# Modulation of a decoder layer: tiles as they arrive, in four column groups

## The chip, the core and the metric

One core of a Trainium2 chip runs one launch of the kernel. The time is the device time of one execution in microseconds. TensorE (PE in the profile, its weight loads PEld) multiplies; VectorE (DVE) and ScalarE (ACT) work element by element; GpSimd (POOL) and SyncE (SP) mostly issue transfers. Each engine works off its own queue in the order in which the program wrote its instructions, and engines wait for each other by semaphores.

## What is computed

One layer of a decoder over 1056 rows (a prompt of 1024, and 8 sequences of 4), in float32. Cut to what the change touches:

```python
mod = (jax.nn.silu(c) @ p['w_mod'] + p['b_mod'])[:, None, :]     # c: 9 x 1024, w_mod: 1024 x 6144
sh_m, sc_m, g_m, sh_f, sc_f, g_f = jnp.split(mod, 6, axis=-1)
h = rmsnorm(x, p['g_pre_mix']) * (1.0 + sc_m) + sh_m
z = h @ p['w_in']                                                # conv | S5 | q | k | v | gates
...
x = x + g_m * rmsnorm(merged @ p['w_out'], p['g_post_mix'])
hf = rmsnorm(x, p['g_pre_ffn']) * (1.0 + sc_f) + sh_f
```

Only shift and scale of the mixer (the first 2048 columns of mod) are needed before the first dense product; the other two thirds are needed much later.

## The kernel before

Features lie on the partitions, rows of x on the free axis, in three chunks of 352. A dense product is float32 in three float32r matmuls: weight and input are each split in a high and a low part (whi, wlo; hh, hl) and high-high, high-low and low-high are added in one PSUM bank. A weight tile (128 x 1024, 512 KB) is loaded by SP into a ring of three raw tiles, split by ScalarE (whi, line 415) and VectorE (wlo, line 416), and used by three atoms of 24 matmuls, one for each chunk.

The program is a list of atoms, written out in order. run() (line 371) walks through it; before an atom's matmuls it emits the splits and loads that are due. loadable() lets loads run three units ahead of the splits, ready() lets splits run two units ahead of the atoms. An atom's evacuation is emitted behind the next atom's matmuls. Then side.advance() emits steps of side generators (depthwise convolution, attention, sample attention, the S5 preparation), paced by the atoms' cost numbers.

The modulation: w_mod is cut into 12 groups of 512 columns with four tiles of 128 x 1024 each (two blocks of the contraction side by side).

- **First groups 0 to 3** (first_mod, line 541). Tiles come into a ring of six buffers, and each gives two float32 matmuls with 9 stationary columns (cs1) and 512 moving ones; the profile lists a float32 matmul as two instructions, its two passes. After four tiles ScalarE copies the 9 x 512 row, and turn_mod (line 561) transposes it in four pieces and adds the bias.
- **Groups 4 to 11** (mod_atoms, line 569). A tile is a unit like any weight: loaded into the raw ring, split in whi and wlo, then four float32r matmuls of 18 stationary columns (high and low of silu(c), c18). A finished group is copied (line 575), turned by four transposes (line 577), and added up by VectorE. add_mod() puts the 32 units singly between the weights' atoms, by some_mods(), gate_jobs() and conv_job(), down to the S5 stage; after the last, a plain atom may stand between a group's end and its turn.

The entry is ordered by the lists FS and FT (line 683): first_sq squares a chunk of x on ScalarE and adds eight blocks to one on VectorE in three steps; first_stats sums over the partitions by matmuls with a column of ones (four sums of 88 rows each) and takes the reciprocal root in 13 small VectorE instructions; first_norm multiplies (3.15 us of VectorE); first_h applies scale and shift and splits into hh and hl. An entry (c, step, (n, i)) of FS puts the step for chunk c behind first tile i of group n. FT's places are counted by chunk and job of the first three dense weights (conv gate, conv value, first branch gate), which run chunk by chunk. The split of the first weight is emitted once the first modulation is through, that of the second ahead of FT, that of the third at the first dense atom, behind the steps at (0, -1).

SP's queue holds all weight loads, x and the first tiles, in order. A load of the first ring waits until the tile six before it has been used.

## Time and profile before

| | us |
|---|---|
| three runs | 1964.32, 1967.68, 1968.45 |
| median | 1967.68 |
| the profiled execution, its own time | 1960.91 |
| its span, first to last instruction | 1958.8 |
| TensorE busy in the span | 1863.8 |
| VectorE, ScalarE busy | 1337.6, 734.4 |
| mean granted TensorE clock | 0.982 |

The profiled execution lies 6.8 us below the median. A timeline row gives the start and length of a run of like instructions, and in brackets how long the engine stood idle before it and what ended that. Matmuls overlap, so the distance between starts tells their pace; lengths contain the end of the last one.

### The profile page before, as it was taken

To read this page: it belongs to the slowest core of one execution; us is meant where nothing else is said; L and a number is where in the kernel's file an instruction comes from. 1 tells how busy PE (TensorE), PEld (TensorE's weight loads), DVE (VectorE), ACT (ScalarE), POOL (GpSimd) and SP (SyncE) were. 2 spreads that over 40 slices of the span, in tenths; PEclk is the share of its full clock that TensorE was granted. 3 is DMA by queue.
4 is the path that set the end of the run, shared out by engine and by line. 5 is a ranking of instruction groups with operands and counts; after the bars stand their busy time and mean duration, and the time that the engine had idled before them with its cause. 6 is when DMAs were issued, how large, how long until landed. Compare 5 with 4: busy or idle time off the path is not lost. (4 is left out here: it accounts for less than half of the span.)

```text
span 1958.8 us, 33717 instructions
## 1 busy us (share of the span) xinstructions
PE 1863.8 (95%) x13512; PEld 1742.9 (89%) x13512; DVE 1337.6 (68%) x2747; ACT 734.4 (37%) x1442; POOL 230.3 (12%) x386
## 2 busy tenths in 40 slices
PE   8899999999899899999899999999999999999995
PEld 2899799789786789999799999989999999999994
DVE  4777686366366677665786668767777777666786
ACT  3422432432431443222233455434333333464452
POOL 0000001001010023222200001100000000110123
PEclk9999999999999999999999999999999999999997
DMA  7333133223247454324843345542322232685654
GB/s 285 102 104 103 60 108 130 91 98 134 101 143 285 167 177 144 100 96 136 238 134 97 122 159 168 205 162 95 109 99 93 82 117 93 207 274 181 228 189 147
DMA packets 89277, 282.29 MB, mean 144 GB/s; under 512 B 16000, under 2 KB 22240, under 8 KB 86944
## 3 DMA queue, kind: packets, MB, share of 16 engines
q1 hardware_dynamic: 51824, 138.49, 22.1%
q0 software_dynamic: 29952, 115.17, 16.8%
q10 hardware_dynamic: 7344, 26.47, 4.1%
q8 instruction: 106, 1.74, 0.4%
q14 instruction: 51, 0.42, 0.1%
HBM read 212.86 MB, written 68.15 MB: 143 GB/s over the span
## 5 line engine op out<-in xcount | busy, mean ns | idle before, releaser
L308 PE MATMUL z<-mh,wop 128*128 128x264 f32 x2032 | 394.7, 286 | 5.2 <-DVE wop L2051 3.0
L308 PE MATMUL z<-hh,whi 128*128 128x352 f32 x1152 | 379.6, 329 | 3.8 <-ACT whi L415 2.3
L308 PE MATMUL z<-hh,wlo 128*128 128x352 f32 x1152 | 373.0, 324 | 3.1 <-DVE wlo L416 3.1
L308 PE MATMUL z<-hl,whi 128*128 128x352 f32 x1152 | 372.6, 323 | 1.1 <-DVE hl L311 1.1
L308 PE MATMUL z<-ml,wop 128*128 128x264 f32 x1400 | 341.5, 286 | 6.3 <-DVE ml L311 6.2
L308 PEld LDWEIGHTS z<-mh,wop 128*128 128x128 f32 x2032 | 326.6, 191 | 7.1 <-DVE wop L2051 4.2
L416 DVE SCALAR_TENSOR_TENSOR wlo<-raw,whi 128x1024 fp32r<-128x1024 f32 x132 | 160.9, 1222 | 131.1 <-ACT whi L415 124.1
L308 PEld LDWEIGHTS z<-ml,wop 128*128 128x128 f32 x1400 | 242.4, 190 | 7.2 <-DVE ml L311 7.1
L308 PEld LDWEIGHTS z<-hh,whi 128*128 128x128 f32 x1152 | 218.6, 190 | 15.0 <-issue 6.3
L308 PEld LDWEIGHTS z<-hh,wlo 128*128 128x128 f32 x1152 | 218.5, 190 | 3.7 <-DVE wlo L416 3.7
L308 PEld LDWEIGHTS z<-hl,whi 128*128 128x128 f32 x1152 | 218.8, 190 | 3.1 <-DVE hl L311 2.0
L415 ACT ACTIVATE whi<-raw 128x1024 fp32r<-128x1024 f32 x132 | 139.2, 1056 | 180.0 <-PE z L308 164.1
L1534 DVE SCALAR_TENSOR_TENSOR ycv<-cub,vecs,ycv 128x1024 f32<-128x1024 f32 x120 | 153.9, 1282 | 3.1
L2047 ACT ACTIVATE wop<-raw 128x512 fp32r<-128x512 f32 x150 | 91.3, 616 | 148.3 <-PE z L308 117.1
L308 PE MATMUL z<-xa,wop 128*128 128x264 f32 x792 | 108.2, 285 | 0.7 <-DVE wop L2051 0.7
L308 PEld LDWEIGHTS z<-xa,wop 128*128 128x128 f32 x792 | 100.9, 189 | 1.0 <-DVE wop L2051 0.9
L311 DVE TENSOR_TENSOR wop<-raw,wop 128x512 fp32r<-128x512 f32 x90 | 61.9, 688 | 44.5 <-ACT wop L2047 44.4
L308 PE MATMUL z<-mh,whi 128*128 128x264 f32 x288 | 85.8, 298 | 1.3 <-DVE ft L2085 0.7
L308 PE MATMUL z<-ml,whi 128*128 128x264 f32 x288 | 83.1, 288 | 0.0
L308 PE MATMUL z<-mh,wlo 128*128 128x264 f32 x288 | 82.8, 288 | 0.0
L308 PE MATMUL z<-zh,whi 128*128 128x264 f32 x256 | 73.6, 287 | 0.0
L308 PE MATMUL z<-zl,whi 128*128 128x264 f32 x256 | 72.8, 284 | 0.0
(438 smaller groups left out, 3663.1 us busy)
## 6 DMA issues: line engine op xcount, KB each, us to landing
raw<-i_win SPq DMA_DIRECT2D x48, 512.0 KB, 3.6
raw<-i_wfi SPq DMA_DIRECT2D x43, 512.0 KB, 4.1
raw<-i_wfo SPq DMA_DIRECT2D x80, 256.0 KB, 3.3
fd<-ft POOLq DMA_DIRECT2D x22, 792.0 KB, 6.8
raw<-i_wmod SPq DMA_DIRECT2D x32, 512.0 KB, 4.1
gd<-g ACTq DMA_DIRECT2D x24, 528.0 KB, 2.9
g<-gd ACTq DMA_DIRECT2D x24, 528.0 KB, 4.7
ml<-fd POOLq DMA_DIRECT2D x22, 528.0 KB, 6.7
```

Source lines behind the costliest of these rows:

```text
L308: return pe.matmul(out=out, lhsT=lhsT, rhs=rhs, start=start, stop=stop, **kw)
L311: dve.tensor_tensor(out=out, in0=a, in1=b, op=op)
L415: act.activation(out=hi[:, 0:n], in_=raw[:, 0:n], func=AF.Copy, scale=scale)
L416: dve.scalar_tensor_tensor(out=lo[:, 0:n], in0=raw[:, 0:n], scalar=scale, in1=hi[:, 0:n].bitcast(F32), op0=ALU.mult, op1=ALU.subtract)
L1534: dve.scalar_tensor_tensor(out=a_, in0=ub[:, k:k + TP], scalar=wv[:, k:k + 1], in1=a_, op0=ALU.mult, op1=ALU.add)
L2047: act.activation(out=w[:, 0:n], in_=src, func=AF.Copy, scale=scale)
```

## The change

- A tile of the modulation is used as it arrives, in float32, without a split (units with asis). mod_mm gives each of two halves of 256 columns and each of two contraction blocks its own 32 output partitions (0, 32, 64, 96), so four matmuls, eight instructions, of 32 stationary columns go to four column groups of the array. 23 of the 32 stationary columns belong to neighbours and their results are not used.
- A group's turn becomes two float32 matmuls of the copied 128 x 256 row against a constant (C_SUM) that adds the two contraction blocks and turns at once.
- The raw tile stays occupied until its matmuls; loadable() holds back the load that would take its place.
- Placement of the 32 later tiles: two behind each gate weight of the attention stages instead of one, one or two more behind the value weights (some_mods(1 + g // 2)), none after the third attention group. All are through before the S5 preparation, whose tables now share the row's memory (pw).
- The entry: chunk 0 is loaded behind the second tile instead of the third, chunk 1 behind the fourth atom instead of the fifth; squares, sums and norms move in FS; the norm of chunk 1 goes from FS to FT, behind the first h. For chunks 0 and 1 the eight blocks of squares are no longer added by VectorE; first_stats gives all eight to the matmuls.

```diff
--- before.py
+++ after.py
@@ -51,7 +51,8 @@
 C_ID, C_ONE = 0, 128
-NCST = 256
+C_SUM = 256
+NCST = C_SUM + 18
@@ -76,6 +77,9 @@
     cst = np.zeros((128, NCST), f)
     cst[:, C_ID:C_ID + 128] = np.eye(128)
     cst[:, C_ONE:C_ONE + 128] = 1.0
+    for r in range(4):
+        for i in range(9):
+            cst[32 * r + i, C_SUM + 9 * (r // 2) + i] = 1.0
     sel = np.zeros((96, 2, 128), f)
     for g in range(3):
         for p in range(2):
@@ -382,7 +386,7 @@
         def load(v):
             src, n, scale, op, keep = units[v]
-            if op:
+            if op and not op.get('asis'):
                 op['load']()
                 return
             raw = wp.tile([128, 1024], F32, tag="raw", name="raw")
@@ -393,12 +397,17 @@
             op = units[v][3]
             if units[v][4]:
                 return ()
+            if op and op.get('asis'):
+                return ()
             return (('whi', 'wlo')[op['no'] % 2],) if op else ('whi', 'wlo')
         def split(v):
             src, n, scale, op, keep = units[v]
             for t in tags(v):
                 rings[t].append(v)
+            if op and op.get('asis'):
+                parts[v] = raws.pop(v)
+                return
             if op:
                 flush()
                 if v + 1 < len(units) and units[v + 1][3]:
@@ -420,10 +429,14 @@
         def ready(v, i):
             if any(len(rings[t]) >= 3 and last[rings[t][-3]] >= i for t in tags(v)):
                 return False
-            ahead = 6 if units[v][3] else 2
+            ahead = 6 if units[v][3] and not units[v][3].get('asis') else 2
             return v < ahead or first[v - ahead] <= i
-        def loadable():
+        def loadable(i):
+
+            v = nd - 3
+            if 0 <= v < len(units) and units[v][3] and units[v][3].get('asis') and last[v] >= i:
+                return False
             return nd < len(units) and nd < ns + (units[nd][3]['ahead'] if units[nd][3] else 3)
         for i, a_ in enumerate(atoms):
@@ -431,12 +444,12 @@
                 a_.pre()
             if i >= start[0]:
                 while ns < len(units) and ready(ns, i) and (i >= start[-1] or i in start[1:] and ns == 0):
-                    while loadable():
+                    while loadable(i):
                         load(nd)
                         nd += 1
                     split(ns)
                     ns += 1
-                while loadable():
+                while loadable(i):
                     load(nd)
                     nd += 1
             if a_.units:
@@ -503,7 +516,7 @@
     ks_ = sc_.tile([128, 3, 2, 32], F32, name="ks_")
     vm = sc_.tile([128, 768], F32, name="vm")
     vs_ = vm[0:32].rearrange("p (g x) -> p g x", g=3)
-    mrow = vm[64:82, 0:512]
+    pw = sc_.tile([128, 512], F32, name="pw")
     cvp_, close_cv = open_pool("cv", side="right", bufs=1)
     mp, close_mp = open_pool("mp", side="right", bufs=1)
     cT = mp.tile([128, 8, 9], F32, name="cT")
@@ -524,7 +537,7 @@
     for i in range(6):
         load_mw(i)
-        if i == 2:
+        if i == 1:
             load_x(0)
     act.dma_start(out=cst, in_=I['cst'])
     act.dma_start(out=vecs, in_=I['vecs'])
@@ -532,67 +545,61 @@
     act.activation(out=cth, in_=cT, func=AF.Tanh, scale=0.5)
     cs2 = mp.tile([128, 8, 9], F32, name="cs2")
     dve.scalar_tensor_tensor(out=cs2, in0=cth, scalar=1.0, in1=cT, op0=ALU.add, op1=ALU.mult)
-    c18 = sc_.tile([128, 8, 18], F32R, name="c18")
-    act.activation(out=c18[:, :, 0:9], in_=cs2, func=AF.Copy)
-    TT(c18[:, :, 9:18], cs2, c18[:, :, 0:9].bitcast(F32), ALU.subtract)
-    cs1 = mp.tile([128, 8, 9], F32, name="cs1")
-    dve.tensor_scalar(out=cs1, in0=cs2, scalar1=0.5, scalar2=None, op0=ALU.mult)
+    cs1 = sc_.tile([128, 96], F32, name="cs1")
+    dve.memset(cs1[:, 72:96], 0.0)
+    dve.tensor_scalar(out=cs1[:, 0:72], in0=flat(cs2), scalar1=0.5, scalar2=None, op0=ALU.mult)
+
+    def mod_mm(s, w, kk):
+
+
+        for half in range(2):
+            for k2 in range(2):
+                r, k = 64 * half + 32 * k2, kk * 2 + k2
+                c0 = k2 * 512 + half * 256
+                mm(s[r:r + 32, 0:256], cs1[:, 9 * k:9 * k + 32], w[:, c0:c0 + 256], kk == 0, kk == 3)
+
+    def mod_turn(n, s, row):
+        for i in range(2):
+            mm(s[:, 256 + i * 18:256 + (i + 1) * 18], row[:, i * 128:(i + 1) * 128], cst[:, C_SUM:C_SUM + 18], True, True)
+        TT(mod[:, 4 * n:4 * n + 4, :].rearrange("p (h i) x -> p h i x", h=2),
+           s[:, 256:292].rearrange("p (i h x) -> p h i x", i=2, h=2),
+           vecs[:, V_BMOD + 4 * n:V_BMOD + 4 * n + 4].rearrange("p (h i) -> p h i", h=2).unsqueeze(3).to_broadcast(
+               [128, 2, 2, 9]), ALU.add)
     def first_mod(n, kk):
         def emit(_):
             if kk == 0:
                 mws['s', n] = zt()
-            s = mws['s', n]
             i = 4 * n + kk
-            w = mws.pop(i)
-            for k2 in range(2):
-                k = kk * 2 + k2
-                mm(s[0:9, :], cs1[:, k, :], w[:, k2 * 512:(k2 + 1) * 512], k == 0, k == 7)
+            mod_mm(mws['s', n], mws.pop(i), kk)
             load_mw(i + 6)
             if kk == 1 and n:
                 turn_mod(n - 1)
         def finish(_):
-            mws['row', n] = mp.tile([9, 512], F32, tag="row", name="row", bufs=2)
-            act.activation(out=mws['row', n], in_=mws['s', n][0:9, :], func=AF.Copy)
+            mws['row', n] = mp.tile([128, 256], F32, tag="row", name="row", bufs=2)
+            act.activation(out=mws['row', n], in_=mws['s', n][:, 0:256], func=AF.Copy)
         atoms.append(Atom([], 1.7, emit, finish if kk == 3 else None))
     def turn_mod(n):
-        row = mws.pop(('row', n))
-        s = mws.pop(('s', n))
-        for i in range(4):
-            pe.transpose(out=s[:, i * 9:(i + 1) * 9], in_=row[:, i * 128:(i + 1) * 128], identity=ident[0:9, 0:9])
-        TT(mod[:, 4 * n:4 * n + 4, :], s[:, 0:36].rearrange("p (i x) -> p i x", i=4),
-           vecs[:, V_BMOD + 4 * n:V_BMOD + 4 * n + 4].unsqueeze(2).to_broadcast([128, 4, 9]), ALU.add)
+        mod_turn(n, mws.pop(('s', n)), mws.pop(('row', n)))
     def mod_atoms(n):
         box = {}
         def finish(_):
-            s = box['s']
-            act.activation(out=mrow, in_=s[0:18, :], func=AF.Copy)
-            for i in range(4):
-                pe.transpose(out=s[:, i * 18:(i + 1) * 18], in_=mrow[:, i * 128:(i + 1) * 128],
-                             identity=ident[64:82, 64:82])
-            t3 = s[:, 0:72].rearrange("p (i x) -> p i x", i=4)
-            tm = sc_.tile([128, 4, 9], F32, tag="mtm", name="mtm", bufs=2)
-            TT(tm, t3[:, :, 0:9],
-               vecs[:, V_BMOD + 4 * n:V_BMOD + 4 * n + 4].unsqueeze(2).to_broadcast([128, 4, 9]), ALU.add)
-            TT(mod[:, 4 * n:4 * n + 4, :], tm, t3[:, :, 9:18], ALU.add)
+            row = pw[:, 0:256]
+            act.activation(out=row, in_=box['s'][:, 0:256], func=AF.Copy)
+            mod_turn(n, box['s'], row)
         out = []
         for kk in range(4):
             def emit(w, kk=kk):
                 if kk == 0:
                     box['s'] = mt()
-                s = box['s']
-                hi, lo = w[0]
-                for k2 in range(2):
-                    k = kk * 2 + k2
-                    mm(s[0:18, :], c18[:, k, :], hi[:, k2 * 512:(k2 + 1) * 512], k == 0, False)
-                    mm(s[0:18, :], c18[:, k, :], lo[:, k2 * 512:(k2 + 1) * 512], False, k == 7)
+                mod_mm(box['s'], w[0], kk)
                 return None
             out.append((flat(I['wmod'][n, kk]), emit, finish if kk == 3 else None))
         return out
@@ -600,8 +607,8 @@
     def add_mod(m):
         if atoms[-1].tag == 'mod' and atoms[-1].evac:
             plain(lambda: None)
-        u = unit(m[0], 1024, 0.5)
-        atoms.append(Atom([u], 0.9, m[1], m[2], tag='mod'))
+        u = unit(m[0], 1024, 1.0, dict(asis=True, ahead=3))
+        atoms.append(Atom([u], 0.3, m[1], m[2], tag='mod'))
     hpool, close_h = open_pool("hpool", bufs=1)
     hh = hpool.tile([128, 8, T], F32R, name="hh")
@@ -650,12 +657,15 @@
     dgs, sqs = [], []
     def first_stats(c):
-        dgs.append(rstd_bcast(mp, [sqs.pop()[:, 0, :]], 1024, EPS))
+        sq = sqs.pop()
+        dgs.append(rstd_bcast(mp, [sq[:, k, :] for k in range(8 if c < 2 else 1)], 1024, EPS))
     def first_sq(c):
         sq = mp.tile([128, 8, CH], F32, tag="sq", name="sq", bufs=1)
         act.activation(out=sq, in_=xcs[c], func=AF.Square)
         sqs.append(sq)
+        if c < 2:
+            return
         TT(sq[:, 0:4], sq[:, 0:4], sq[:, 4:8], ALU.add)
         TT(sq[:, 0:2], sq[:, 0:2], sq[:, 2:4], ALU.add)
         TT(sq[:, 0], sq[:, 0], sq[:, 1], ALU.add)
@@ -680,10 +690,10 @@
         for i, a in enumerate((hh, hl)):
             act.activation(out=hs2[:, :, i * 32:i * 32 + 32], in_=a[:, :, TP:T].bitcast(F32), func=AF.Copy)
-    FS = ((0, first_sq, (0, 2)), (0, first_stats, (1, 0)), (0, first_norm, (1, 2)), (1, load_x, (1, 0)),
-          (1, first_sq, (2, 2)), (1, first_stats, (3, 0)), (1, first_norm, (3, 2)))
-    FT = ((1, first_h, (0, -1)), (2, first_sq, (0, 1)), (2, first_stats, (1, 0)), (2, first_norm, (1, 1)),
-          (2, first_h, (1, 1)))
+    FS = ((0, first_sq, (0, 0)), (1, load_x, (0, 3)), (0, first_stats, (1, 1)), (1, first_sq, (2, 0)),
+          (0, first_norm, (2, 1)), (1, first_stats, (3, 0)))
+    FT = ((1, first_norm, (0, -1)), (1, first_h, (0, -1)), (2, first_sq, (0, 1)), (2, first_stats, (1, 0)),
+          (2, first_norm, (1, 1)), (2, first_h, (1, 1)))
     for n in range(4):
         for i in range(4):
             first_mod(n, i)
@@ -1184,7 +1194,8 @@
         yield 2.0
         tmp1, tmp2 = t16(), t16()
-        PW = sc_.tile([128, 2, 9, 16], F32, name="PW")
+        assert not mods
+        PW = pw[:, 0:288].rearrange("p (r s t) -> p r s t", r=2, s=9)
         dve.memset(PW[:, 0, 0, :], 1.0)
         dve.memset(PW[:, 1, 0, :], 0.0)
         TT(PW[:, 0, 1, :], mag, co, ALU.mult)
@@ -1232,7 +1243,7 @@
         yield 2.0
         cmul_small(5, 4, 4)
-        WK = sc_.tile([128, 7, 2, 16], F32, name="WK")
+        WK = pw[:, 288:512].rearrange("p (i r t) -> p i r t", i=7, r=2)
         def csq(orr, oi, ar, ai):
             TT(tmp1, ai, ai, ALU.mult)
@@ -1673,17 +1684,18 @@
             conv_job(1, 1)
             conv_start(1)
         v_atoms(g)
+        some_mods(1 + g // 2)
         plain(lambda: None)
         plain(lambda g=g: P_.update({('gen', g): side.add(att_gen(g))}))
         if g < 2:
             conv_job(g + 2, 1)
-        gate_jobs(GA[g], 1)
+        gate_jobs(GA[g], 2)
         if g < 2:
             conv_start(g + 2)
         plain(lambda: None)
         plain(lambda g=g: side.finish(P_['gen', g]))
     plain(lambda: (P_.update(cg=side.add(combine_gen())), side.add(s5_prep())))
-    gate_jobs(GC, 1)
+    gate_jobs(GC, 0)
     plain(lambda: (side.finish(P_['cg']), P_['close_ap'](), close_cv(), open_ub(), side.add(ln_gen()),
                    side.add(sample_gen())))
     gate_jobs(GS, 0)
```

## Rows read from the trace of the kernel before

**Rows 1.** The page, part 1: busy us (share of span) xinstructions of each engine.
```profile
PE 1863.8 (95%) x13512; PEld 1742.9 (89%) x13512; DVE 1337.6 (68%) x2747; ACT 734.4 (37%) x1442; POOL 230.3 (12%) x386
```

**Rows 2.** Stages: us, busy us (x) by engine, TensorE clock, DMA share, GB/s.
```profile
10.00:20.00 10.00, 9.68 (x28) 2.27 (x26) 4.52 (x13) 3.14 (x2) 0.00 (x0) 1.00 1.01 411
...
45.50:48.90 3.40, 3.15 (x11) 3.14 (x11) 2.20 (x7) 2.83 (x5) 0.00 (x0) 0.50 0.65 214
...
240.00:243.40 3.40, 3.40 (x22) 2.74 (x20) 3.32 (x5) 0.78 (x3) 0.00 (x0) 0.51 0.66 154
...
496.00:502.80 6.80, 5.12 (x24) 2.95 (x25) 2.29 (x17) 4.34 (x20) 0.00 (x0) 0.50 0.00 1
```

**Rows 3.** Timeline: start us, us, what, xcount [idle before <-releaser]; TensorE, entry.
```profile
5.48 11.64 PE L308 MATMUL z<-mw,cs 128*9 128x512 f32 x20 [5.48 <-DMA mw<-i_wmod]
...
28.48 5.32 PE L308 MATMUL z<-mw,cs 128*9 128x512 f32 x12
...
33.73 0.79 PE L308 MATMUL s<-cst,sq 128*88 128x1 f32 x8
...
39.21 1.88 PE L308 MATMUL z<-mw,cs 128*9 128x512 f32 x4
```

**Rows 4.** Timeline of ScalarE and VectorE, entry, chunk 1 and its chain.
```profile
25.31 2.53 ACT L657 ACTIVATE sq<-xc 128x2816 f32<-128x2816 f32 x1
...
28.77 3.10 DVE L311 TENSOR_TENSOR sq<-sq 128x1408 f32<-128x1408 f32 x3
...
34.56 0.16 DVE L466 TENSOR_SCALAR rs_v<-s 88x4 f32<-88x4 f32 x1 [2.68 <-PE s L308]
...
41.42 3.15 DVE L311 TENSOR_TENSOR xc<-xc,s 128x1408 f32<-128x1408 f32 x2
...
56.58 1.23 DVE L416 SCALAR_TENSOR_TENSOR wlo<-raw,whi 128x1024 fp32r<-128x1024 f32 x1
```

**Rows 5.** Timeline of TensorE: the first dense matmuls that wait.
```profile
45.75 0.66 PE L308 MATMUL z<-hh,wlo 128*128 128x352 f32 x1 [2.45 <-DVE wlo L416]
...
56.60 0.43 PE L308 MATMUL z<-hh,whi 128*128 128x352 f32 x1 [1.78 <-ACT whi L415]
...
57.86 0.43 PE L308 MATMUL z<-hh,wlo 128*128 128x352 f32 x1 [0.67 <-DVE wlo L416]
```

**Rows 6.** Timeline of TensorE over one middle tile, from dense to dense.
```profile
100.75 0.32 PE L308 MATMUL z<-hh,wlo 128*128 128x352 f32 x1
...
101.84 0.32 PE L308 MATMUL z<-hh,whi 128*128 128x352 f32 x1
```

**Rows 7.** Timeline of TensorE: matmuls in two row groups, in two column groups.
```profile
226.99 0.32 PE L308 MATMUL z<-hh,wlo 128*128 128x352 f32 x1
227.24 1.13 PE L308 MATMUL s<-K,Q 64*128 64x256 f32 x8
228.31 0.93 PE L308 MATMUL s<-PT,V 128*64 128x128 f32 x12
...
751.11 2.18 PE L308 MATMUL s<-U,Gin 128*64 128x144 f32 x32
753.22 0.43 PE L308 MATMUL z<-hh,whi 128*128 128x352 f32 x1
```

**Rows 8.** The page, parts 5 and 6: the splits; loads with KB, us to landing.
```profile
L415 ACT ACTIVATE whi<-raw 128x1024 fp32r<-128x1024 f32 x132 | 139.2, 1056 | 180.0 <-PE z L308 164.1
...
raw<-i_win SPq DMA_DIRECT2D x48, 512.0 KB, 3.6
```

**Rows 9.** Tile m: who waited for the groups turned by L577, us in total, times.
```profile
  PE m L577: 3.7, 3
```

**Rows 10.** Timeline of TensorE: the starts of attention groups 1 and 2.
```profile
350.31 0.71 PE L840 MATMUL s<-cst,P 128*128 128x128 f32 x2 [2.91 <-ACT P L829]
...
497.69 0.48 PE L840 MATMUL s<-cst,P 128*128 128x128 f32 x1 [4.17 <-ACT P L829]
```

**Rows 11.** Timeline of TensorE: sums near the end, at the 1.2 GHz clock.
```profile
1943.40 1.02 PE L308 MATMUL s<-cst,ss 128*88 128x1 f32 x6
```

## Prediction

> **What bounds the kernel now.** I read the page first: TensorE is busy for 95% of the span [rows 1], so a microsecond of its work counts wherever it doesn't wait, and an engine that is relieved gives nothing unless TensorE waited for it. The change touches two places, and each has its own limit. The entry, 0 to 58 us, is read by the stages' table and the three engines' timelines [rows 2 to 5]. There TensorE looks busy until 41 us with the sixteen first tiles [rows 3], but dense work does not flow when they are done. From 34.56 us VectorE works off one chain almost without a pause: the second chunk's reciprocal root, half of the modulation and of h, the norm of chunk 1 (3.15 us at 41.42), the first weight's low part, the other half, h of chunk 1, and at 56.58 the low part of the third weight [rows 4]. TensorE takes two weights' matmuls from 45.75 to 54.82, then stands 1.78 and 0.67 us until that third weight is split [rows 5]. So the entry ends with VectorE's chain, 23.3 us from 34.56 to 57.8, and the chain starts with the squares of chunk 1, not with the modulation. The 32 tiles of the layer's middle (100 to 792 us) stand mostly in a stream of dense matmuls without a gap; there I read TensorE's timeline around one tile [rows 6].
>
> **The tiles in the middle.** Before, a tile costs four 512-column matmuls, 1.09 us from one dense start to the next over it [rows 6], where a dense matmul starts every 0.16. After, it is eight of 256 columns, two passes for each of four column groups. One such pass by itself takes half of the 0.437 us that a 512-column one takes (5.25 us for twelve) [rows 3], 0.22. No row shows four groups at once. Two do run side by side: thirty-two matmuls in two column groups of 64 take 2.11 us to the next start, 0.132 for a pair of 144 columns, of which each alone takes 0.123; eight of 256 columns in two row groups take 1.32 us from dense start to the next work, four steps of 0.22 and 0.45 around them [rows 7]. Four at once are two steps: 0.44 + 0.45 = 0.89. With the lesser overhead of the thirty-two (the same 0.25 to enter, then 2.11 - 16 x 0.123 = 0.14) they are 0.83. I take 0.87, nearer to the row with 256 columns: 0.22 saved, times 32 = **-7.0** (-6.4 to -8.3). If only two run at once the tile costs 0.44 more, 1.31.
>
> The Trainium skill, in TensorE: Matmul & The Clock Gate, "Measured speedup vs the span model", gives 2.38 times for three column groups; scaled to four, an estimate of 3.2 times. The matmuls of a tile would take 1.75 / 3.2 = 0.55 instead of 0.44, and the sum below would be 3.5 us worse. The pairs here come nearer to their full factor than that, and no run here shows four.
>
> ScalarE and VectorE lose the splits, 1.06 us [rows 8] and the low part (1.2 us, as at 56.58 [rows 4]) per tile. In the dense stream TensorE didn't wait for them: nothing on the path. A raw tile is now held until its matmuls are done, so the dense weight three units on is loaded only then: 3.6 us to land, 1.06 and 1.2 to split, done 5.9 us after the tile, where it is first used some 12 us after it (one dense weight and a tile). Covered with 6 us to spare; without that cover each would cost up to 5.9. Behind the waiting split on ScalarE stands the row copy of a finished group. For groups 4 and 6 (of 4 to 11) the turn follows one dense chunk (24 x 0.16 = 3.9 us), while the copy is ready at 3.6 + 1.06 + about 0.6: 1.4 us wait each. Groups 7, 8 and 11 turn straight behind their last tile, some 1.1 each. Together 6.1, the other three groups none; before it was 3.7 in three waits [rows 9], and one was followed by 3.4 us at 1.2 GHz [rows 2], worth 1.7. **+0.7** (-3.7 to +4).
>
> **Tiles moved into waits.** At the starts of attention groups 1 and 2 TensorE waits 2.91 and 4.17 us for ScalarE's P [rows 10], held by the mask table that GpSimd's queue loads late. The change puts one tile with its turn (0.9 + 1.1) and two tiles (1.7) between the values' matmuls and this start. GpSimd's queue doesn't pass by them, so the table comes as before and the waits shrink by up to 3.7; the tiles' loads share the transfers with the table, so I take **-3.1** (0 to -3.7). After the second wait the clock is 1.2 GHz for 6.8 us [rows 2]; with shorter waits I count half of such a stretch less, **-1.7** (0 to -5). In exchange a tile that stood among the sample's waits near 712 us leaves: **+0.9**. The other late tiles come out of dense stretches at their price.
>
> **The entry.** The sixteen tiles shrink from 1.75 us (4 x 0.437) to about 0.6, and then the transfers set the pace: 411 GB/s at 10 to 20 us [rows 2], 512 KB per tile and 1408 KB per chunk. Chunk 0 is loaded behind the second tile instead of the third, chunk 1 behind the tenth instead of the eleventh. Tile 13, after which the sums of chunk 1 stand on TensorE before and after, lands at 5.5 + (12 x 0.524 + 2 x 1.442) MB / 0.411 = 27.8 us. VectorE's three additions (3.10 us [rows 4]) had cover before, so taking them away saves nothing there; they become 32 sums of two matmuls each, 64 against 8. Eight take 0.79 us, the last one's 0.22 included, so their starts stand (0.79 - 0.22) / 7 = 0.08 apart [rows 3]: 64 x 0.08 = 5.1 us at 2.4 GHz. At 1.2 GHz it is (1.02 - 0.29) / 5 = 0.146 [rows 11]: 9.4 us. So the chain's start moves from 34.5 to 33.0 or to 37.3. The norm of chunk 1 only changes its place within VectorE's chain, behind the first two splits; the splits wait for ScalarE 0.5 more. The chain then ends at 56.8 to 61.1 against 57.8. But TensorE gets its first two weights 4 us earlier in the good case and is through by about 52, so it idles some 5 us rather than 2.5, and before, the wait of 2.45 us that ended at 45.75 was followed by 3.4 us at 1.2 GHz [rows 2, 5]: 1.7 more. Entry: -1.0 + 1.7 = +0.7 up to 3.3 + 1.7 = +5.0. Which clock the sums get can't be read from a row, since TensorE was busy without a pause there; I take about the middle, **+2.5**.
>
> The Trainium skill, same page, "LDWEIGHTS (loading the stationary operand)", gives columns / 1.2 ns whatever the clock: 88 columns, 73 ns, so 64 sums would take 4.7 us and the entry +0.4 to +0.7 either way. The rows differ: 80 ns at one clock and 146 at the other [rows 3, 11], and the measurement decides.
>
> **Sum.** -7.0 + 0.7 - 3.1 - 1.7 + 0.9 + 2.5 = -7.7. The profiled execution's 1960.91 (span 1958.8) becomes 1953.2; the median shown, 1967.68, is 6.8 above that execution, so I forecast 1967.68 - 7.7 = **1960.0**, by itself 1956 to 1964.
>
> **The rivals.**
> *The entry follows the modulation.* If VectorE's chain is not what ends it, the tiles' end decides, 41.0 to 35.4, or -5.6 instead of +2.5: 1951.9. For it: TensorE has no gap until 41. Against: the waits at 56.60 and 57.86.
> *TensorE stays at 1.2 GHz through the entry.* Both sums take 9.4: chunk 0's ends at 26 instead of 22, the tiles behind it release their buffers late, tile 13 is used at 33, the chain starts at 42.9: +8.4 + 1.7, or 7.6 above the forecast: 1967.6.
> *Slower: only two column groups at a time.* Place: every tile of the middle. Price: 0.44 x 32 = 14.1: 1974.1. It decides from a tile of 1.11 us, which is 2.6 groups at a time. For it: only pairs are shown, and a group's two passes stand ahead of the next group in program order. Against: the pairs in the rows overlap although their program order, too, puts one group's matmuls first.
> *No overlap at all*, so that it doesn't do what it says: tile 0.45 + 1.75 = 2.2, +42, and the entry some 5 more: 2007.
> *Three of four* (the factor 3.2): 1963.5.
> *The held raw tiles hurt*: a split that comes late by 1 us for most dense weights of the middle, +9: 1969.
>
> **How the numbers follow.** Forecast 0.45, entry faster 0.10, entry at 1.2 GHz 0.17, two groups 0.11, none 0.04, three of four 0.06, late splits 0.07. About 0.2%, 3.9 us, can be told from no change: faster below 1963.8, slower above 1971.6. Faster: 0.42 of the forecast, 0.10, 0.04 of three of four: 0.56. Slower: 0.11 + 0.04, 0.03 of the slow entry, 0.02 of the late splits: 0.20. Same: 0.24. The range takes in the entry's gain and most of the two-group case, 1951 to 1974; outside are no overlap and the tails, some 0.15.
>
> **What would show it.** A dense start to dense start of 0.85 to 0.89 us over a tile, with four groups' matmuls within some hundredths. The 64 sums' length, and the granted clock there. VectorE's third low part at 56 to 61, TensorE idle before it, then at 1.2 GHz. Waits under 2 and 3 us at the attention starts. A tile over 1.1 us, or dense matmuls that begin without a wait before 52, makes the forecast wrong.

## The result, and the profile after

The changed kernel takes 1988.2 us, the one before 1966.2: a ratio of 1.0105, 95% interval 1.0086 to 1.0125. It is 22 us slower; 1960.0 was forecast, 1951 to 1974 the range. Its profiled execution has a span of 1991.0, 32 more than that of before, of which some 10 are the place of the two executions among their runs.

The page, part 1 (busy us, share of the span, instructions), beside [rows 1]:

```profile
PE 1877.0 (94%) x13816; PEld 1768.1 (89%) x13816; DVE 1294.6 (65%) x2701; ACT 699.8 (35%) x1409; POOL 230.5 (12%) x386
```

VectorE and ScalarE are relieved by 43 and 35 us, as the change says. TensorE, which bounds the kernel, is busy 13 us longer, although 32 tiles got shorter: it ran more of its work at 1.2 GHz (its mean granted clock is 0.970, before 0.982). The stages' table (us, busy us by engine, TensorE clock, DMA share, GB/s), beside [rows 2]:

```profile
36.00:39.30 3.30, 3.30 (x45) 3.16 (x41) 0.84 (x1) 0.03 (x1) 0.00 (x0) 1.00 0.70 209
39.40:56.40 17.00, 14.59 (x77) 11.89 (x77) 10.42 (x28) 7.38 (x11) 0.00 (x0) 0.50 0.43 150
503.60:507.00 3.40, 3.40 (x26) 2.17 (x30) 0.93 (x8) 2.10 (x10) 0.00 (x0) 0.50 0.00 0
558.20:568.40 10.20, 6.06 (x27) 5.68 (x28) 3.03 (x4) 2.83 (x5) 1.74 (x3) 0.50 0.63 216
```

**The entry**, beside [rows 3 to 5]: the timeline (start us, us, engine, line, operation, count, idle time before), of TensorE, ScalarE and VectorE.

```profile
5.50 1.08 PE L312 MATMUL z<-mw,cs 128*32 128x256 f32 x8 [5.50 <-DMA mw<-i_wmod]
...
12.50 1.08 PE L312 MATMUL z<-mw,cs 128*32 128x256 f32 x8 [3.62 <-DMA mw<-i_wmod]
...
18.23 9.53 PE L312 MATMUL s<-cst,sq 128*88 128x1 f32 x64
...
27.68 3.64 PE L312 MATMUL z<-mw,cs 128*32 128x256 f32 x32
...
29.96 2.54 ACT L665 ACTIVATE sq<-xc 128x2816 f32<-128x2816 f32 x1
...
36.15 6.78 PE L312 MATMUL s<-cst,sq 128*88 128x1 f32 x64
...
42.97 0.16 DVE L479 TENSOR_SCALAR rs_v<-s 88x4 f32<-88x4 f32 x1 [6.13 <-PE s L312]
...
65.28 0.43 PE L312 MATMUL z<-hh,whi 128*128 128x352 f32 x1 [3.80 <-ACT whi L424]
...
66.54 0.59 PE L312 MATMUL z<-hh,wlo 128*128 128x352 f32 x1 [0.67 <-DVE wlo L425]
```

A tile is short, and TensorE waits for the next to land. The first 64 sums start 0.147 us apart, the pace at 1.2 GHz in [rows 11]. The four tiles behind them begin only at 27.68; ScalarE, which copies a finished row ahead of the next squares, and the one buffer for squares wait for that, so the squares of chunk 1 start at 29.96 instead of 25.31. Their sums begin at 2.4 GHz, go on at 1.2 from 39.3 and end at 42.9. VectorE's chain starts at 42.97, not 34.56, and the third weight's low part is waited for until 66.54, not 57.86. Until 56.4 dense work runs at 1.2 GHz. At 86 us the kernel is 10.4 us behind.

**A middle tile**, beside [rows 6], TensorE:

```profile
111.69 0.64 PE L312 MATMUL m<-raw,cs 128*32 128x256 f32 x8
...
123.66 0.32 PE L312 MATMUL z<-hh,wlo 128*128 128x352 f32 x1
123.91 0.64 PE L312 MATMUL m<-raw,cs 128*32 128x256 f32 x8
124.48 0.43 PE L312 MATMUL z<-hh,whi 128*128 128x352 f32 x1
124.75 0.32 PE L312 MATMUL z<-hl,whi 128*128 128x352 f32 x1
```

and before, from tile to tile:

```profile
100.92 0.40 PE L308 MATMUL m<-whi,c 128*18 128x512 f32 x1
...
113.30 0.40 PE L308 MATMUL m<-whi,c 128*18 128x512 f32 x1
```

Dense start to dense start is 0.82 us instead of 1.09. But the second dense matmul comes 0.27 after the first instead of 0.16, so a weight with its tile takes 12.22 us (111.69 to 123.91, tile to tile) instead of 12.38 (100.92 to 113.30): 0.16 saved, not 0.27.

**The third attention group** (from 487 us, beside [rows 9, 10]), all engines and SP:

```profile
357.22 1.49 PE L850 MATMUL s<-cst,P 128*128 128x128 f32 x4 [0.33 <-ACT P L839]
...
502.35 1.61 PE L850 MATMUL s<-cst,P 128*128 128x128 f32 x4 [1.55 <-ACT P L839]
...
508.58 0.43 PE L312 MATMUL z<-hh,whi 128*128 128x352 f32 x1 [0.85 <-ACT whi L424]
509.83 0.43 PE L312 MATMUL z<-hh,wlo 128*128 128x352 f32 x1 [0.67 <-DVE wlo L425]
...
554.27 1.07 PE L312 MATMUL m<-raw,cs 128*32 128x256 f32 x16
554.68 1.04 ACT L424 ACTIVATE whi<-raw 128x1024 fp32r<-128x1024 f32 x1
...
554.97 8.66 SPq L393 DMA_DIRECT2D raw<-i_win  x4
...
560.96 1.06 ACT L424 ACTIVATE whi<-raw 128x1024 fp32r<-128x1024 f32 x1 [4.88 <-DMA raw<-i_win]
561.93 0.37 ACT L594 ACTIVATE pw<-m 128x256 f32<-128x256 f32 x1
...
562.34 1.04 PE L312 MATMUL m<-cst,pw 128*128 128x18 f32 x4 [7.01 <-ACT pw L594]
```

The waits at the attention starts shrank as forecast. But the last two tiles hold two of the three raw tiles; the next weights' loads are issued at 554.97, when the tiles are used. ScalarE waits until 560.96 for the weight that it has to split, the row's copy stands behind this split, and TensorE waits 7.01 us for the last group's turn. 10.2 us at 1.2 GHz surround that wait.

**Late stages.** Who waited (total us, times, longest), TensorE: 650 to 780 us, where the S5 stage begins, and 900 to 952:

```profile
PE s L1347 <- DVE GT L315: 2.6, 2, 1.3
...
PE s L312 <- DMA Tm<-Mt: 4.3, 2, 2.8
```

**The whole way.** An instruction that stands in both traces comes 10.4 us later in the changed kernel at 86 us, 6.9 and 4.7 at the two attention starts (350.31 and 357.22, 497.69 and 502.35), 18.3 at ScalarE's table load behind the third group (586.06 and 604.38) and 27.1 at VectorE's mrg behind the S5 stage (957.96 and 985.03). From there both run alike to 1704 us of before; then the distance grows to 31.2 by 1782 and 32.2 at the end. The program of these last stages is the same in both, and e15 and e12 below, which differ in the entry alone, move apart there by as much: it is scatter between executions.

### The profile page after: what moved, and what is told of

The parts are those of the page before. It is cut to its first block, busy times and chain, and to the rows that moved or that the text cites. A ratio compares the mean times of both kernels' runs of the same rounds, so it can differ in the third digit from the quotient of the medians.

```text
span 1991.0 us, 34178 instructions
## 1 busy us (share of the span) xinstructions
PE 1877.0 (94%) x13816; PEld 1768.1 (89%) x13816; DVE 1294.6 (65%) x2701; ACT 699.8 (35%) x1409; POOL 230.5 (12%) x386
## 3 DMA queue, kind: packets, MB, share of 16 engines
q8 instruction: 108, 1.77, 0.4%
## 5 line engine op out<-in xcount | busy, mean ns | idle before, releaser
L312 PE MATMUL z<-hh,whi 128*128 128x352 f32 x1152 | 386.9, 336 | 6.5 <-ACT whi L424 5.1
L312 PE MATMUL z<-hl,whi 128*128 128x352 f32 x1152 | 376.6, 327 | 0.5 <-DVE hl L315 0.5
L312 PEld LDWEIGHTS z<-mh,wop 128*128 128x128 f32 x2032 | 326.6, 190 | 10.1 <-DVE wop L2063 5.3
L312 PEld LDWEIGHTS z<-hh,whi 128*128 128x128 f32 x1152 | 222.8, 193 | 23.1 <-issue 12.1
L312 PEld LDWEIGHTS z<-hl,whi 128*128 128x128 f32 x1152 | 223.0, 194 | 1.1 <-DVE hl L315 0.7
L425 DVE SCALAR_TENSOR_TENSOR wlo<-raw,whi 128x1024 fp32r<-128x1024 f32 x100 | 122.2, 1222 | 123.2 <-ACT whi L424 122.8
L424 ACT ACTIVATE whi<-raw 128x1024 fp32r<-128x1024 f32 x100 | 105.5, 1055 | 121.4 <-PE z L312 76.8
```

The costliest lines, as they stand in the source:

```text
L312: return pe.matmul(out=out, lhsT=lhsT, rhs=rhs, start=start, stop=stop, **kw)
L424: act.activation(out=hi[:, 0:n], in_=raw[:, 0:n], func=AF.Copy, scale=scale)
L425: dve.scalar_tensor_tensor(out=lo[:, 0:n], in0=raw[:, 0:n], scalar=scale, in1=hi[:, 0:n].bitcast(F32), op0=ALU.mult, op1=ALU.subtract)
```

## The experiments

All compute the whole layer, and each ratio is against the kernel before on the same chip.

### Halves of the change undone

*e1_entry*: the entry of before. *e2_sums*: VectorE's additions put back. *e3_place*: the places of before. *e4_both*: e1 and e3.

```diff
 # e1_entry: FS, FT, load_x(0), first_mod, turn_mod, first_sq, first_stats as before
 # e2_sums
-        dgs.append(rstd_bcast(mp, [sq[:, k, :] for k in range(8 if c < 2 else 1)], 1024, EPS))
+        dgs.append(rstd_bcast(mp, [sq[:, k, :] for k in range(1)], 1024, EPS))
-        if c < 2:
-            return
 # e3_place (PW and WK in memory of their own)
-        some_mods(1 + g // 2)
-        gate_jobs(GA[g], 2)
+        gate_jobs(GA[g], 1)
-    gate_jobs(GC, 0)
+    gate_jobs(GC, 1)
```

> The changed kernel with the whole entry of the kernel before (9 x 512 first tiles and their turns, loads, order of squares, sums and norms, VectorE's additions); the 32 middle tiles, their turns and places stay changed. The changed trace stands 10.4 us behind the one before when the third dense weight is reached (86.17 against 75.82). Theory A, the entry costs its own 10 us and the rest of the loss arises later: 1988 - 10 = 1978, dense work without a wait from about 58, TensorE's clock 2.4 GHz from about 11 us. Rival B, what is lost in the entry is given back later (later waits shrink because transfers are further ahead): 1984 to 1988.

> The changed kernel with VectorE's three additions of the squares put back for chunks 0 and 1, so 4 sums for a chunk instead of 32; short first tiles, loads and order stay changed. Theory A1, the 64 matmuls for each chunk (9.53 and 6.78 us in the changed trace, at 1.2 GHz) are the entry's loss: the chain on VectorE starts near 34 instead of 42.97, and 7 to 9 us come back: 1979 to 1981. Rival A2, the short first tiles leave TensorE at 1.2 GHz and that is the loss, whatever sums it: the first dense matmuls still run at 1.2 GHz, VectorE's additions take the place of the sums, and at most 4 come back: 1984 or more.

> The changed kernel with the 32 middle tiles in the places of the kernel before (one behind each gate weight, none behind the values, six in the sample's and the S5 stage). Theory C, four tiles of which two stand behind one gate weight of the third attention group hold the raw ring, the next weights load late and the turn of group 11 waits 7.0 us and is followed by 10.2 us at 1.2 GHz: without it 8 to 9 us come back, while the waits at the two attention starts, 0.33 and 1.55 us now, grow again to 2.9 and 4.2 (+4): 1988 - 9 + 4 = 1983. Rival D, the longer time at 1.2 GHz between 590 and 770 us and the waits near 945 also come from the places: 7 to 10 more, 1974 to 1977. Rival E, the places don't matter: 1988.

> The changed kernel with both the entry and the places of the kernel before: against the kernel before only the middle tiles' form is changed. In the changed trace a weight with a tile behind it takes 12.22 us instead of 12.38, since the second dense matmul behind a tile is late by 0.11 too. Theory F, a tile saves 0.16 us and nothing else is different: 1966.2 - 32 x 0.16 = 1961. Rival G, it saves the 0.27 that stand between the dense starts around it (0.82 against 1.09): 1957.7. Rival H, raw tiles held until their matmuls make later weights' splits late: 1966 or more.

Measured: e1 1975.6 (1.0048, 1.0025 to 1.0071), e2 1978.0 (1.0071), e3 1968.6 (1.0017, 1.0003 to 1.0032), e4 1956.7 (0.9955, 0.9938 to 0.9972). By the medians the entry costs 12.7 (11.2 by the ratios) and most of that are the sums: A and A1 hold. The places cost 19.6 (17.3), more than the wait of 7.0 explains and more than C, D and E said. Together 31.5 (29.5), so the two add up. What is left, the tile's new form, gains 8.8 us (5.5 to 12). G's 8.5 lies in that interval, F's 5.1 just outside, H falls. Not all of it is the tile itself. The two attention starts, beside [rows 10], in e3 and then in e4, where every tile stands where it stood before:

```profile
356.35 1.48 PE L850 MATMUL s<-cst,P 128*128 128x128 f32 x4 [2.08 <-ACT P L839]
...
498.59 1.63 PE L850 MATMUL s<-cst,P 128*128 128x128 f32 x4 [1.78 <-ACT P L839]
```
```profile
347.34 1.63 PE L856 MATMUL s<-cst,P 128*128 128x128 f32 x4 [1.88 <-ACT P L845]
...
492.21 1.48 PE L856 MATMUL s<-cst,P 128*128 128x128 f32 x4 [0.69 <-ACT P L845]
```

The waits of 2.91 and 4.17 us shrank in both, without a tile moved to them.

### What makes the sums dear

*e5_long*: only the first tiles long again. *e9_fill*: twelve more matmuls, read by nobody, behind each short tile. *e13_sums*: on top of e11_best (below), only the 64 sums.

```diff
 # e9_fill
-            mod_mm(mws['s', n], mws.pop(i), kk)
+            w = mws.pop(i)
+            if i == 0:
+                mws['sink'] = mt()
+            mod_mm(mws['s', n], w, kk)
+            for j in range(3):
+                for r in range(0, 128, 32):
+                    mm(mws['sink'][r:r + 32, 0:256], cs1[:, r // 32:r // 32 + 32], w[:, 2 * r:2 * r + 256], True, True)
 # e13_sums, against e11_best
-        dgs.append(rstd_bcast(mp, [sq[:, k, :] for k in range(1)], 1024, EPS))
+        dgs.append(rstd_bcast(mp, [sq[:, k, :] for k in range(8 if c < 2 else 1)], 1024, EPS))
+        if c < 2:
+            return
```

> The changed kernel with only the sixteen first tiles put back to 9 x 512 (and their turns by four transposes); loads, order and the 32 sums for a chunk stay changed. In the changed trace the clock is 1.2 GHz until 35.93 us and again from 39.34 to 56.41; with VectorE's additions put back (the run before) 9 us of the entry came back although the clock there stayed low. Theory A1, the number of sums: they cost 64 x 0.08 = 5.1 us at least at any clock, but long tiles lengthen TensorE's queue ahead of them, so little comes back: 1984 to 1988. Theory A2, the low clock is the consequence of the short tiles and makes the sums dear: with long tiles they take about 5.1 us each instead of 9.53 and 6.78, and the first dense matmuls run at 2.4 GHz (2.8 us): 1979 to 1981.

> The changed kernel with work added that nobody reads: behind each short first tile twelve more matmuls of the same shape (three times the tile's) into a spare PSUM bank, so that TensorE is busy for about as long as with the long tiles. Theory A2: the clock rises to 2.4 GHz early in the entry, the sums take 5.1 us each, and the kernel gets faster by up to 8 although it does more: 1980 to 1984. Theory A1: the sums' number is the loss and the added 16 x 1.3 us of matmuls make it no better: 1988 or more.

> The same as the first run of this four but with the eight blocks of squares of chunks 0 and 1 summed by 64 matmuls each instead of by VectorE and 8; long tiles, loads and order as before. In the last runs the clock fell to 1.2 GHz 2.4 to 3.8 us after such a row of one-column matmuls had begun, with TensorE never idle, also with long tiles ahead of it. Theory S, the row itself lowers the clock: it takes 6 to 8 us, the tiles behind it and the first dense matmuls run at 1.2 GHz, and the chain starts 6 to 8 us late: 1960 to 1963. Rival, at 2.4 GHz: 5.1 us against VectorE's 3.1 and 0.8, +1.2: 1955.

Measured: e5 1993.1 (1.0132), e9 1993.6 (1.0136), e13 1965.3 (1.0005, 0.9990 to 1.0020) against 1954.3 without the 64 sums. A2 falls: with TensorE busy without a pause and at 2.4 GHz ahead of the sums, the two rows still take 7.50 + 7.01 us (e5) and 6.20 + 7.50 (e9), where A2 had 5.1 each and the changed kernel has 9.53 + 6.78; and neither run is faster. The stages of e13 show why; the sums begin at 17.46 and 41.34:

```profile
17.50:21.90 4.40, 4.40 (x58) 4.40 (x57) 0.00 (x0) 0.00 (x0) 0.00 (x0) 1.00 1.05 421
22.00:28.70 6.70, 6.70 (x19) 2.15 (x18) 2.69 (x15) 0.00 (x0) 0.00 (x0) 0.50 0.52 199
29.00:41.30 12.30, 12.30 (x32) 2.64 (x30) 3.35 (x3) 3.61 (x3) 0.00 (x0) 1.00 0.63 191
41.40:45.80 4.40, 4.40 (x58) 4.40 (x57) 0.00 (x0) 0.00 (x0) 0.00 (x0) 1.00 0.23 88
45.90:52.60 6.70, 6.70 (x18) 2.14 (x18) 3.73 (x18) 1.00 (x2) 0.00 (x0) 0.50 0.16 44
```

And TensorE's timeline of e13:

```profile
17.46 5.65 PE L312 MATMUL s<-cst,sq 128*88 128x1 f32 x64
```

Both rows of sums begin at 2.4 GHz, and 4.5 us into each the clock falls, with TensorE busy in every moment. The tiles behind them run at half pace: the third dense weight's low part is there at 71.60 us in e13, at 57.95 in e11, and in e11 the clock stays at 2.4 GHz from 9 to 46 us:

```profile
9.00:46.00 37.00, 31.90 (x100) 8.36 (x99) 21.63 (x49) 10.92 (x11) 0.00 (x0) 1.00 0.75 285
```

Theory S holds, and the cost is larger than its 6 to 8: 11 us (12.6 by the ratios).

### Short tiles and order in the entry

*e12_short*: e11_best with short first tiles. *e15_order*: e12 with the changed loads and lists FS and FT. Both keep VectorE's additions.

> The same as the run above but with the sixteen first tiles in four column groups; loads, order and VectorE's additions as before. Theory A2', short tiles alone leave TensorE at 1.2 GHz (with VectorE's additions and short tiles the clock was 1.2 GHz from 25.5 to 46 and 56 to 63 us): dense work runs at half pace for up to 7 us, 3 to 4 us more than above: 1958. Rival: the tiles' end comes earlier (1.75 to 0.6 us each) and VectorE's chain starts earlier, which makes up for it: 1950 to 1954.

> Short first tiles, VectorE's additions put back, five tiles in the S5 stage, but loads and the order of squares, sums and norms as changed: against the run with short tiles and the order of before (1951.5) only loads and order differ. Theory O1, the order and the earlier loads cost nothing by themselves and the sums were the whole loss of the entry: 1950 to 1954. Rival O2, the norm of chunk 1 behind the first splits and h, late in VectorE's queue, makes the third weight's low part and h of chunk 1 late: 1955 to 1959.

Measured: e12 1951.5 (0.9924, 0.9907 to 0.9941), e15 1956.3 (0.9958, 0.9941 to 0.9974). Short tiles gain some 3 us, though the clock of e12 is at 1.2 GHz from 29.4 to 49.8 us:

```profile
29.40:49.80 20.40, 15.75 (x72) 10.77 (x73) 16.01 (x35) 8.84 (x14) 0.00 (x0) 0.50 0.54 196
```

VectorE's chain starts at 32.70 us instead of 34.66 in e11, and the third weight's low part is there 1.96 us earlier too; TensorE waits for this chain anyway. A2' falls.

With the changed loads and order TensorE waits 3.94 and 0.67 us for the third weight, 0.49 and 0.67 in e12, but most of this is only that it gets through the first two weights sooner. The low part of the third weight in e12, the same in e15, and the stage behind it in e15:

```profile
55.99 0.43 PE L312 MATMUL z<-hh,wlo 128*128 128x352 f32 x1 [0.67 <-DVE wlo L425]
```
```profile
56.60 0.66 PE L312 MATMUL z<-hh,wlo 128*128 128x352 f32 x1 [0.67 <-DVE wlo L425]
```
```profile
56.40:59.70 3.30, 3.10 (x10) 3.10 (x11) 1.73 (x2) 1.68 (x1) 0.00 (x0) 0.50 0.54 163
```

It is 0.6 us late, 3.4 us at 1.2 GHz follow, and at the first middle tile e15 is 2.4 us behind (101.50 against 99.11). The timed runs say 5 us (6.7 by the ratios), in O2's range; but the rest of the distance between the two traces comes behind 900 us, where their programs are the same. Both differences of this section are near what the runs resolve.

### The places

*e6_turn*: every turn put off behind the next dense weight. *e16_turn11*: only the last one. *e7_late*: in the third attention group one tile a gate and none behind the values, five in the S5 stage. *e14_gc*: these five behind the gate weights between. *e17_single* and *e18_pairs*: only the gates' second tiles, only the values' pair moved there. *e11_best*: e7 with the entry of before. In all of them the tables of the S5 preparation have memory of their own.

```diff
 # e7_late
-        some_mods(1 + g // 2)
+        some_mods((1, 1, 0)[g])
-        gate_jobs(GA[g], 2)
+        gate_jobs(GA[g], (2, 2, 1)[g])
 # e14_gc: e7, and
-    gate_jobs(GC, 0)
+    gate_jobs(GC, 1)
-    gate_jobs(GS, 0)
+    gate_jobs(GS, 1)
 # e16_turn11: group 11's finish()
-    gate_jobs(GC, 0)
+    gate_jobs(1, 0)
+    plain(lambda: turns[0](None))
+    gate_jobs(GC - 1, 0)
```

> The changed kernel with the turns of the 32 middle tiles put off: the row is copied ahead of the last chunk of the next dense weight and turned behind it, so no turn stands behind a split that waits for its load; tables of the S5 preparation have their own memory. All tiles keep their places. Theory C1, the turns are the loss of the places: the waits of 0.50, 1.77 and 7.01 us and the time at 1.2 GHz behind the last two go: 1988 - 12 = 1976. Rival C2, the weights that come late behind held raw tiles are the loss, and TensorE only waits for them one step later: 1985 to 1988.

> The changed kernel with only the last group's turn put off, behind the first gate weight after the third attention group (no further group needs the bank, so nothing waits behind it); tables with their own memory. The five tiles taken out of the third group gave some 15 (1988.2 to 1973.3). Theory C1, the turn behind the late split is most of that: its 7.0 us and the 3 us lost at 1.2 GHz behind it come back: 1978. Theory C2, the weights that load late behind held raw tiles are the loss, and TensorE waits for them one step later: 1984 or more.

> The changed kernel with the places of its first two attention groups, but in the third one tile behind each gate weight and none behind the values, so that five tiles stand in the S5 stage again, as before; tables with their own memory. All places undone gave 1968.6. Theory D1, the loss lies in the third group's pairs (7.0 us wait and its clock) and in the uncovered waits of the S5 stage: nearly as good as all undone, 1967 to 1972. Rival D2, the tiles in the first two attention groups cost as well: 1976 or more.

> The changed kernel with the places of the run that put five tiles back into the S5 stage, but these five now one behind each gate weight of the two stages ahead of it (three and two), so that none is left in the S5 stage; entry as changed. That run gave 1966.2. Theory D1a, the third group's pairs are the loss of the places, and the S5 stage needs no tiles: 1966 to 1968. Theory D1b, the tiles in the S5 stage lie beside its waits (7.0 us of waits and 2.9 us lost to the clock near 945 without tiles there, 5.0 and 0 with five): 1971 to 1974.

> The changed kernel, but in the third attention group one tile behind each gate weight instead of two; the three taken out stand one behind each of the next three gate weights. The two behind the values stay. No tiles in the S5 stage, entry as changed, tables with their own memory. Theory P1, the pairs behind the gate weights are the third group's loss (a pair takes two of the three raw tiles, and the weights behind it load only when it is used): about as good as with five tiles taken out, 1973 to 1976. Theory P2, the pair behind the values, ahead of the attention start, carries as much: 1980 or more.

> The changed kernel, but without the two tiles behind the values of the third attention group; the pairs behind its gate weights stay, and two tiles stand behind the next two gate weights. Theory P1: the waits behind the pairs stay, 1984 to 1988; group 10's turn now falls behind the second pair. Theory P2: half of the 15 comes back, 1977 to 1981.

> Entry of the kernel before (long first tiles, VectorE's additions, its order), middle tiles in the new form in the places of the run that kept the first two attention groups' pairs and put five tiles back into the S5 stage. If entry and places add up, as they did (-12.7, -19.6, together -31.5): 1966.2 - 12 = 1954. If the places of the first two groups bring nothing beyond those of the kernel before: 1957, as with all undone.

Measured: e6 1987.0 (1.0100), e16 1989.1 (1.0114; its runs from 1978 to 1993), e7 1966.2 (0.9998, 0.9988 to 1.0008), e14 1973.3 (1.0035), e17 1981.3 (1.0057; three of its eight runs from 1970 to 1972, five from 1981 to 1985), e18 1980.2 (1.0058), e11 1954.3 (0.9941, 0.9925 to 0.9956).

D1, D1b and the adding up of entry and places (e11) came as forecast. C1 does not come in the medians. e6 makes the next group's first tile wait for the bias addition, since there is one bank: it says little. e16 has no such wait and its wait of 7.0 us is gone from the trace. The last pair of tiles and ScalarE's table load behind the group in e16, that load in the changed kernel, and a stage of e16:

```profile
557.44 1.07 PE L312 MATMUL m<-raw,cs 128*32 128x256 f32 x16
...
591.34 1.28 ACT L1198 ACT_TABLE_LOAD   x1 [0.39 <-ACT g L1632]
```
```profile
595.03 1.28 ACT L1192 ACT_TABLE_LOAD   x1 [0.39 <-ACT g L1627]
```
```profile
503.40:513.40 10.00, 9.47 (x49) 6.68 (x50) 2.54 (x10) 4.34 (x15) 0.00 (x0) 0.50 0.50 170
```

At the pair e16 is 3.2 us behind the changed kernel (554.27), at the load 3.7 us ahead: over the place itself the whole 7 us come back. What it loses ahead of that, in the same instructions, goes with 10 us at 1.2 GHz where the changed kernel has 3.4. One of its four runs, 1978.2, is at C1's time. So these runs do not decide whether the wait's 7 us are lost in every execution.

The stretch with the same dense work of the third group, in the changed kernel, in e14, e17 and e18 (each from a stages' table of its own):

```profile
440.11:584.20 144.09, 130.80 (x932) 115.47 (x931) 60.23 (x160) 40.80 (x131) 10.61 (x17) 0.95 0.40 137
```
```profile
439.68:565.96 126.28, 123.19 (x895) 110.24 (x894) 58.97 (x158) 39.76 (x129) 10.60 (x17) 1.00 0.40 136
```
```profile
439.43:570.58 131.15, 127.39 (x911) 112.81 (x911) 58.87 (x158) 39.72 (x129) 10.61 (x17) 0.97 0.40 138
```
```profile
440.10:572.54 132.44, 126.81 (x920) 112.98 (x919) 58.70 (x158) 39.52 (x129) 10.61 (x17) 0.99 0.41 141
```

Idle 13.3 us, 3.1, 3.8 and 5.6; the clock 0.95, 1.00, 0.97, 0.99. Against e14 the stretch is 18 us longer with all five tiles, 6 with the gates' second tiles alone (e18) and 5 with the values' pair alone (e17): together they cost more than one by one. The timed runs say 15 us (13.8 by the ratios) for the five, 7 (4.5) for the gates' second tiles, 8 (4.3) for the values' pair. Both medians lie in P2's ranges and not in P1's, but e17's runs fall in two bunches, of which one is below P1's range, and each single cost is about as large as its uncertainty. The rows show waits for the splits behind pairs and, around all waits, time at 1.2 GHz. How much of the 15 is the one and how much the other stays open.

The S5 stage: e14, without tiles there, is 7 us behind e7. Its waits, as above for the changed kernel (the first two from 650 to 780, the third from 900 to 952):

```profile
PE m L312 <- ACT pw L594: 5.3, 1, 5.3
PE s L1346 <- DVE GT L315: 4.1, 2, 2.8
...
PE s L312 <- DMA Tm<-Mt: 3.3, 2, 1.9
```

In e7 the waits for Tm are gone and those for GT come to 0.4; the trace of before has neither in these stages. The five tiles lay beside VectorE's and the transfers' work, and their absence turns it into waits. The 5.3 us are once more a last turn behind a late split and a cost of e14's own places, so the 7 is not the tiles' cover alone.

### The change put together step by step

| | median, us | ratio (interval) | step, us | first middle tile in the trace, us |
|---|---|---|---|---|
| before | 1966.2 | 1 | | 100.92 |
| e4: middle tiles in the new form | 1956.7 | 0.9955 (0.9938 to 0.9972) | -8.8 | 102.27 |
| e11: places of the first two attention groups | 1954.3 | 0.9941 (0.9925 to 0.9956) | -2.8 | 101.38 |
| e12: first tiles short | 1951.5 | 0.9924 (0.9907 to 0.9941) | -3.3 | 99.11 |
| e15: loads and order of the entry | 1956.3 | 0.9958 (0.9941 to 0.9974) | +6.7 | 101.50 |
| e7: sums by 64 matmuls | 1966.2 | 0.9998 (0.9988 to 1.0008) | +7.9 | 112.16 |
| e14: no tiles in the S5 stage | 1973.3 | 1.0035 (1.0022 to 1.0048) | +7.3 | 108.23 |
| changed: five tiles in the third group | 1988.2 | 1.0105 (1.0086 to 1.0125) | +13.8 | 111.69 |

A step is the difference of the ratios times 1966; its own uncertainty is 4 to 5 us, so the second and third may be nothing. The last column is where the entry ends: e7, e14 and the changed kernel have one and the same entry, so single traces scatter by up to 4 us there. By it the short tiles bring 2.3 us, loads and order cost 2.4, and the sums 10.7. e12 beats both kernels: 15 us under the one before, 37 under the changed one.

## Why the prediction was wrong

**The tiles: the mechanism right, the size partly by luck.** Forecast -7.0, measured -8.8 (-5.5 to -12). 0.87 was named as the dense distance and 0.82 came, but that view misses the second dense matmul, late by 0.11 too; by the trace the tile itself saves 0.16 x 32 = 5.1, not 7.0. The rest lies in shorter waits, which the forecast had put at nothing for the relieved ScalarE and VectorE: TensorE's waits from 90 to 600 us sum to 13.7 before and to 10.9 in e4. All four groups run at once: a second tile right behind the first adds 0.43 us (sixteen instructions take 1.07 us where eight take 0.64), just the two passes of 0.22. The rivals of two groups, of three and of none fall. The Trainium skill, TensorEngine Tiling (Array Packing), "Key Properties", says that changing the tiling mode drains TensorE; the trace agrees, with 0.25 us into the tile and the 0.27 behind it against 0.16.

**Held raw tiles and turns: right for one tile, wrong for pairs.** Behind single tiles no weight is late (no wait of TensorE from 90 to 222 us). The step that failed is "Covered with 6 us to spare" together with the turns "straight behind their last tile, some 1.1 each": both count one held tile and 3.6 us to land. Behind two, two weights are loaded together, the first is there 6.0 us after its issue (554.97 to 560.96), and the last turn took 7.0. The turns' waits, forecast at 6.1 instead of 3.7, came to 0.50 + 1.77 + 7.01 = 9.3, and time at 1.2 GHz stands around the last one. The third group's five tiles cost 14 in all, and that was in no rival: "The held raw tiles hurt" had the mechanism, but put 9 us on the dense weights of the whole middle. How the 14 divide into waits and clock stays open.

**Attention starts: the size came, the mechanism only in part.** 2.91 and 4.17 became 0.33 and 1.55, -5.2 against -3.1 forecast from tiles moved into the waits. But with every tile in its old place the two waits are already 3.9 together (e3) and 2.6 (e4) instead of 7.1: more than half of the gain came with the tile's new form, and why is not shown. The -1.7 for the clock didn't come: 3.4 and 10.2 us at 1.2 GHz in the third group stand against 6.8 [rows 2].

**Late tiles: wrong in place and size.** "+0.9" counted one tile among the sample's waits and took the others out of dense streams at their price. The rows of before showed TensorE without gaps at those tiles because they stood in what else would have been gaps; without them 2.6 + 4.3 us of waits appear, and the step is +7.3. Waits that a step now covers have no row in the trace of before.

**The entry: wrong.** Forecast +2.5, at most +5.0; by the traces +10.4, by the steps -3.3 + 6.7 + 7.9 = +11.3. The step that failed is the price of the sums: "Which clock the sums get can't be read from a row" and then a middle between 5.1 us at 2.4 GHz and 9.4 at 1.2. They took 9.53 and 6.78, and only chunk 1's were priced, though chunk 0's stand in the same queue ahead of tiles, row copies and squares. The row of sums itself takes the clock down (e13), and what stands behind it pays. The rival "TensorE stays at 1.2 GHz through the entry", with a chance of 0.17, came closest: chain start at 42.9 and +10.1 forecast, 42.97 and +10.4 measured. That it hit to a tenth is luck: chunk 1's sums began at 36.15, not at 33.5, and took 6.78, not 9.4. Second, "The norm of chunk 1 only changes its place within VectorE's chain", priced at 0.5, with the earlier loads: 2.4 in the trace's entry, 6.7 by the timed runs, neither clear of the scatter.

The Trainium skill, TensorE: Matmul & The Clock Gate, "LDWEIGHTS (loading the stationary operand)", gives a load's ns as its columns over 1.2, without a term for the clock; an estimate from it is 73 ns for 88 columns, 4.7 us for 64 sums. At 2.4 GHz the runs come near it, 0.078 us from start to start (e13); at 1.2 GHz they do not, 0.147 (9.53 us for the row). By the prediction's own sum the entry at 4.7 us would have been +0.3, not +0.4.

## What to carry to other kernels

Work moved here from a busy-looking helper to the bounding engine was paid there in full, and again by everything queued behind it; before moving such work, ask whether the helper's time was on the path at all. Filler between dense stages hides waits that no trace of the filled kernel shows, so take it out of one stage at a time. Price a held buffer by how many are held together, and test the parts of a change one by one: here three gained some 15 us and four lost some 36. When a run shows a wait gone or grown, look where the engine stands behind it: a longer wait can be an earlier arrival.

## What the hardware showed that was not expected

- A row of 64 weight loads with one-column matmuls lowers TensorE's clock although the engine is never idle: in e13 it falls from 2.4 to 1.2 GHz 4.5 us after each such row began, in e5_long, e9_fill and the changed kernel's second row some 2 to 4 us after; without the rows (e11) it stays at 2.4 GHz.
- Four column groups with float32 matmuls of 256 columns run fully side by side: eight instructions take 0.57 us to the next dense start (123.91 to 124.48), a second tile behind them 0.43 more.
- Behind them the second dense matmul comes 0.27 us after the first instead of 0.16.
